# Side steps behind TensorE's last queued block, spaced by products; two norms' roots moved to VectorE

## The chip, the cores and the metric

The kernel runs on one core of a Trainium2 chip. The metric is the device time of one execution in microseconds (us), taken as the median of several runs. Engines: PE is TensorE (PEld its weight loads), DVE is VectorE, ACT is ScalarE, POOL is GpSimd, SP is SyncE, whose queue issues nearly all DMAs here. L96 means line 96 of the kernel before.

## The reference, cut to what matters

One decoder layer on 512 prompt tokens and 8 x 8 sample tokens (576 columns in all), float32. A normalised input `h` is projected by `w_in` (1024 x 6656) and feeds three branches, which sigmoid gates merge:

```
u = ca * sigmoid(cb);  c = causal_dwconv31(u);  c = silu(layernorm(c));  p_conv = c @ w_conv_out
q,k,v,f -> HGRN2, 4 heads of 128x128 state;  o = rmsnorm(o) * silu(hgate);  p_hg = o @ w_hg_out
s = qm @ mem_k^T / sqrt(128);  om = softmax(s) @ mem_v;  p_mem = om @ w_mem_out
out = (g0*p_conv + g1*p_hg + g2*p_mem) @ w_out        (then RMSNorms and a dense SwiGLU FFN)
```

The sample tokens attend to 8 caches of 256 keys and values per head, which are loaded from HBM.

## The kernel before, in words

Every large product is made of three passes over pairs of rounded high and low parts (`mm3`, L94 to L97), so that PE is the busiest engine. Until about 545 us the kernel works through a list of **tasks** (L1068 to L1097). Most tasks are one **block**: 16 calls of `mm3` (8 rows of weights for each of two groups of 256 and 320 tokens), whose two results lie in two of the four PSUM buffers with the tag `mm` and are then read by ACT or DVE. A `p_conv` or `p_mem` task is 8 calls. The order of tasks that matters here: four convolution inputs, keys and values, four queries (`q_task`), eight `gate_conv`, `hgate(0)`, `hq(0)`, `hf(0)`, `hgate(1..3)`, eight `p_conv`, then the gates and outputs of the memory branch with heads 1 and 2 between them, then `gate_hg` with head 3, then `p_hg`.

Beside the blocks run **side steps**, written as generators: the convolution's taps and its layer norm (`conv_taps`, `conv_tail`, in the queue `convq`), attention of the prompt and the heads (`attn_prompt`, `hg_decay`, `hg_main`, in `side`) and the sample tokens' attention (`attn_sample`, in `sampq`). After each task `pump(conv, ns)` takes `conv` steps from `convq` and `ns` from the two others. This sets the order in which instructions are written down; a planner with costs of its own then orders each engine's queue, taking what it holds to be ready, earlier lines first.

What is named below:

- `conv_tail` (L435): sums over channels (L454 to L456 on DVE, L461 on PE), centring (L465), squares (L468, L471, L472), the variance of each token by ten one-column products (L477, PSUM buffer `ps`), copies (L480, L481), a root `rsqrt` (L133) on POOL, five diagonal tiles on DVE (L487), five products that spread the root over all partitions (L489, PSUM buffers `pr`), and per channel group the scaling (L494, L495), sigmoid (L498), L499, L500 and the split into high and low parts, the first write of which is ACT L102 into a fresh big buffer `hl` (L491).
- `attn_sample` (L628): eight units of key transposes (L643), copies (L644) and scores (L649); the softmax (L597 to L603); transposes of the probabilities (L658, a PSUM buffer `ps`) and their copy (L660); products with the cached values (L671, PSUM buffer `ops`, once per group of four sequences); a copy `oo` (L676), transposes (L679) and splits. The values are loaded by SP (L632), two in advance.
- `hq(0)` takes a big buffer for head 0 (`hg_alloc`, L750); its two results are read by ACT L770 and DVE L771, the latter writing into that big buffer. `hf(0)` writes there as well (ACT L764, L765).
- `hg_main` (L835): head norm with squares (L903), sums (L904), a root on POOL, L909, transposes (L915) and the gated output (L922).
- Pools: `S` (8 big buffers), `x` (5), `tb` (3), and in PSUM `mm` (4) and `sd` (4, for all side products). A tile takes a buffer of its tag's ring at its first write.

Of the kernel before, what the change touches and what calls it, by code (L numbers as in the profile page):

```python
# [42 lines left out]
def tile_decoder_layer(  # L43
# [14 lines left out]
    pps = ctx.enter_context(tc.tile_pool(name="pps", bufs=4, space=PSUM))  # L58
    pd = ctx.enter_context(tc.tile_pool(name="pd", bufs=5, space=bass.MemoryType.DRAM))

    seq, last = [0], {}

    def nm(s):
        seq[0] += 1
# [26 lines left out]
    def f32(ap):  # L91
        return ap.bitcast(F32)

    def mm3(out, whi, wlo, xhi, xlo, start, stop, more=False):  # L94
        T.matmul(out, lhsT=whi, rhs=xhi, start=start, stop=False, skip_group_check=more)  # L95
        T.matmul(out, lhsT=whi, rhs=xlo, start=False, stop=False, skip_group_check=more)  # L96
        last["mm"] = T.matmul(out, lhsT=wlo, rhs=xhi, start=False, stop=stop, skip_group_check=more)  # L97

    def split(hi, lo, src, scale=None, eng=None):

        if scale is None:
            A.activation(hi, src, AF.Copy)  # L102
            (eng or V).tensor_tensor(lo, src, f32(hi), op=ALU.subtract)  # L103
        else:
            ins = A.activation(hi, src, AF.Identity, scale=scale)  # L105
            ins2 = V.scalar_tensor_tensor(out=lo, in0=src, scalar=scale, in1=f32(hi), op0=ALU.mult,  # L106
                                          op1=ALU.subtract)
            return ins, ins2
# [201 lines left out]
    h = (hhi, hlo)  # L310
    convq, side, sampq = deque(), deque(), deque()

    def step(q):
        while q:
            try:
                next(q[0])
                return
            except StopIteration:
                q.popleft()

    def pump(nc_=1, ns=1):
# [12 lines left out]
    g0, g1 = GRP
    junk = big()
# [99 lines left out]
    def conv_tail():  # L435
        last = tmp(512)
        for j in range(4):
            A.activation(last[:, P * j:P * j + 30], uext[:, j, 512:542], AF.Copy)
            A.activation(last[:, P * j + 32:P * j + 96].rearrange("p (b t) -> p b t", b=NB),
                         usamp(j)[:, :, 30:38], AF.Copy)  # L440
        ps, psb = sdb(), sdb()
        for j in range(4):
            T.transpose(ps[:30, P * j:P * j + P], last[:, P * j:P * j + 30], ident)
            T.transpose(psb[:64, P * j:P * j + P], last[:, P * j + 32:P * j + 96], ident)
        l2, l3 = tmp(512), tmp(512)
        A.activation(l2[:30, :], ps[:30, :], AF.Copy)
# [12 lines left out]
        for g in range(2):  # L459
            t0, n = GRP[g]  # L460
            T.matmul(pm[g][:, :n], lhsT=ones, rhs=s[:, t0:t0 + n], start=True, stop=True)  # L461
        for j in range(4):
            for g in range(2):
                t0, n = GRP[g]
                V.tensor_tensor(ca[:, j, t0:t0 + n], ca[:, j, t0:t0 + n], pm[g][:, :n], op=ALU.subtract)  # L465
            if j == 0:
                s = tmp()
                A.activation(s, ca[:, j], AF.Square)  # L468
            else:
                sq = tmp()  # L470
                A.activation(sq, ca[:, j], AF.Square)  # L471
                V.tensor_tensor(s, s, sq, op=ALU.add)  # L472
            yield
        ps = sdb()
        for t in range(5):
            m = P if t < 4 else 64
            T.matmul(ps[:m, 2 * t:2 * t + 1], lhsT=s[:, P * t:P * t + m], rhs=ones[:, 0:1], start=True, stop=True)  # L477
        vs = tiny()
        V.memset(vs, 1.0)
        V.tensor_copy(vs[:, 0:4], ps[:, 0:8].rearrange("p (a b) -> p a b", b=2)[:, :, 0])  # L480
        V.tensor_copy(vs[:64, 4:5], ps[:64, 8:9])  # L481
        r = rsqrt(vs[:, 0:5], 5, 1.0)
        pr = [sdb(), sdb()]
        for t in range(5):
            m = P if t < 4 else 64
            dg = tmp(P)
            V.tensor_scalar(dg[:m, :m], ident[:m, :m], r[:m, t:t + 1], 512.0, op0=ALU.mult, op1=ALU.mult)  # L487
            o = pr[0][:, P * t:P * t + P] if t < 4 else pr[1][:, :64]
            T.matmul(o, lhsT=ones[:m, :], rhs=dg[:m, :m], start=True, stop=True)  # L489
        yield  # L490
        hl = big(FR).rearrange("p (s j t) -> p s j t", s=2, j=4)  # L491
        hi, lo = hl[:, 0], hl[:, 1]
        for j in range(4):
            V.tensor_tensor(ca[:, j, :512], ca[:, j, :512], pr[0], op=ALU.mult)  # L494
            V.tensor_tensor(ca[:, j, 512:], ca[:, j, 512:], pr[1][:, :64], op=ALU.mult)  # L495
            g, b = cT[:, j, 32:33], cT[:, j, 33:34]
            sg = tmp()
            A.activation(sg, ca[:, j], AF.Sigmoid, scale=g, bias=b)  # L498
            V.tensor_scalar(ca[:, j], ca[:, j], g, b, op0=ALU.mult, op1=ALU.add)  # L499
            V.tensor_tensor(ca[:, j], ca[:, j], sg, op=ALU.mult)  # L500
            split(hi[:, j], lo[:, j], ca[:, j])
            yield
        chl.append((hi, lo))
# [124 lines left out]
    def attn_sample():  # L628
# [29 lines left out]
                T.transpose(ps[:, 256 * g + P * mh:256 * g + P * mh + P], pr[:, g, P * mh:P * mh + P], ident)  # L658
        pT = xtile()[:, :512]
        A.activation(pT, ps, AF.Copy)  # L660
        yield
        for g in range(2):
            ops = sdb()
            for j in range(4):
                vj, u = vcs.popleft(), 4 * g + j + 2
                if u < 8:
                    vcs.append(load(cache_mem_v, *units[u]))
                for mh in range(2):
                    for b in range(4):
                        c = 256 * g + P * mh + 32 * b  # L670
                        T.matmul(ops[32 * b:32 * b + 32, P * j:P * j + P], lhsT=pT[:, c:c + 32],  # L671
                                 rhs=vj[:, 2 * b + mh, :], start=mh == 0, stop=mh == 1)
                if j % 2:
                    yield
            oo = tmp(512)
            A.activation(oo, ops, AF.Copy)  # L676
            ps = sdb()
            for j in range(4):
                T.transpose(ps[:, P * j:P * j + P], oo[:, P * j:P * j + P], ident)  # L679
            c0 = SEQ + 32 * g  # L680
            for j in range(4):
                src = ps[:, P * j:P * j + P].rearrange("p (b i t) -> p b i t", b=4, i=4)[:, :, j, :]
                hi, lo = (mem["om"][:, s, j, c0:c0 + 32].rearrange("p (b t) -> p b t", b=4) for s in range(2))
                split(hi, lo, src)
            yield
# [87 lines left out]
    def hg_decay(j):  # L773
# [56 lines left out]
        A.activation(d["kEs"][64:, :], ps[64:, :P], AF.Copy)  # L830
        d["scaled"] = scaled
        G.memset(d["sc"], 0.0)
        yield

    def hg_main(j):  # L835
        d = hg[j]
# [11 lines left out]
        for t in range(4):  # L848
# [3 lines left out]
            else:  # L852
# [11 lines left out]
        vm = tmp(512)  # L864
        V.tensor_tensor(vm[64:].rearrange("p (b v) -> p b v", b=4), vs.unsqueeze(1).to_broadcast([64, 4, P]),
                        m4[64:].unsqueeze(2).to_broadcast([64, 4, P]), op=ALU.mult)
        yield
        ps = sdb()
        for t in range(4):
            c = P * t  # L870
# [33 lines left out]
        V.reduce_sum(ss[:, 0:4], sq.rearrange("p (t v) -> p t v", t=4), axis=AX.X)  # L904
        sq = tmp(P)
        A.activation(sq[:64, :], obs[:64, :P], AF.Square, accum_out=ss[:64, 4:5])
        r = rsqrt(ss[:, 0:5], 5, 1.0 / P)
        on = d["on"]
        V.tensor_tensor(on[:, :512].rearrange("p (t v) -> p t v", t=4), ob.rearrange("p (t v) -> p t v", t=4),  # L909
                        r[:, 0:4].unsqueeze(2).to_broadcast([P, 4, P]), op=ALU.mult)  # L910
        V.tensor_scalar(d["ons"][:64, :], obs[:64, :P], r[:64, 4:5], None, op0=ALU.mult)
        yield
        pT, pTs = sdb(), sdb()
        for t in range(4):
            T.transpose(pT[:, P * t:P * t + P], on[:, P * t:P * t + P], ident)  # L915
# [2 lines left out]
        if j == 0:  # L918
# [3 lines left out]
        V.scalar_tensor_tensor(out=og[:, :512], in0=pT, scalar=g, in1=gt[:, :512], op0=ALU.mult, op1=ALU.mult)  # L922
        V.scalar_tensor_tensor(out=og[:, 512:], in0=pTs[:, :64], scalar=g, in1=gt[:, 512:], op0=ALU.mult,
                               op1=ALU.mult)
        split(hg["og"][:, 0, j], hg["og"][:, 1, j], og)
        yield

        Ds = PP[:, 512:576].rearrange("p (b t) -> p b t", b=NB)[:, :, 7]
# [17 lines left out]
    def win(c):  # L946
        return wcols(w_in, c, P)
# [111 lines left out]
        return norm_group(xtb, 0, hhi, hlo, *g1, junk=junk[:, D:2 * D], eng=A, fills=8)  # L1059

    def hgate(j):
        add(hg_task(j), win(C_HG + P * j), ns=4)

    def hf(j):
        add(hq_task(j), win(C_HQ + P * j), ns=4)
        add(hf_task(j), win(C_HF + P * j), ns=4)

    for j in range(4):  # L1068
        add(conv_task(j), win(C_CB + P * j), win(C_CA + P * j), conv=1)
# [9 lines left out]
    for j in range(1, 4):  # L1079
        hgate(j)  # L1080
    for n in range(8):
        add(p_conv(n), *([wcols(w_conv_out, P * n, 256)] if n % 2 == 0 else []), conv=2, ns=3)
    for n in range(0, 8, 2):
        add(gate_mem(n), win(C_GL + 2 * D + P * n), ns=4)
        add(gate_mem(n + 1), win(C_GL + 2 * D + P * n + P), ns=4)
        add(p_mem(n), wcols(w_mem_out, P * n, 256), ns=3)
        add(p_mem(n + 1), ns=3)
# [467 lines left out]
```

## Time and profile before

| | us |
|---|---|
| median of 3 runs (1004.88 to 1005.20) | 1005.19 |
| the profiled execution | 1005.55 |
| its span from first to last instruction | 1003.8 |
| PE busy in it | 986.9 |
| DVE, ACT, POOL busy | 693.3, 433.5, 33.5 |

The profiled execution is 1.75 us longer than its span. A timeline row gives start, length, engine, line, operation, tiles, shapes, the number of merged instructions, and in brackets how long the engine stood idle before it and what ended that. Since matmuls overlap, a busy PE can still be slower than PE at its peak.

### The profile page before, as it was taken

To read this page: it belongs to the slowest core of one execution; us is meant where nothing else is said; L and a number is where in the kernel's file an instruction comes from. 1 tells how busy PE (TensorE), PEld (TensorE's weight loads), DVE (VectorE), ACT (ScalarE), POOL (GpSimd) and SP (SyncE) were. 2 spreads that over 40 slices of the span, in tenths; PEclk is the share of its full clock that TensorE was granted. 3 is DMA by queue.
4 is the path that set the end of the run, shared out by engine and by line. 5 is a ranking of instruction groups with operands and counts; after the bars stand their busy time and mean duration, and the time that the engine had idled before them with its cause. 6 is when DMAs were issued, how large, how long until landed. Compare 5 with 4: busy or idle time off the path is not lost.

```text
span 1003.8 us, 16880 instructions
## 1 busy us (share of the span) xinstructions
PE 986.9 (98%) x6915; PEld 924.0 (92%) x6915; DVE 693.3 (69%) x1235; ACT 433.5 (43%) x766; POOL 33.5 (3%) x127
## 2 busy tenths in 40 slices
PE   8999999999899999999999999999999999999997
PEld 7997899889699999999999779999999999999995
DVE  6689997485875365566548788878777876813715
ACT  6544346574621232223234466344444544614612
POOL 1120000000101001001000000000000000000000
PEclk9999999999999999999999999999999999999999
DMA  8415421543743222222323615023232333321302
GB/s 244 140 64 194 121 80 47 148 132 107 207 134 95 84 85 75 76 87 65 95 77 134 181 64 178 1 85 114 77 104 85 96 115 137 139 81 54 128 20 95
DMA packets 125931, 106.55 MB, mean 106 GB/s; under 512 B 3208, under 2 KB 110244, under 8 KB 125846
## 3 DMA queue, kind: packets, MB, share of 16 engines
q1 hardware_dynamic: 125854, 105.48, 33.9%
q8 instruction: 54, 0.88, 0.4%
q14 instruction: 23, 0.19, 0.1%
HBM read 97.15 MB, written 8.68 MB: 105 GB/s over the span
## 4 chain that ended last, share of the span: by engine, by line
PE 82%; DVE 7%; DMA 5%; ACT 2%; issue 2%; POOL 1%; SPq 0%; DVEq 0%; ACTq 0%
PE mm L96 18%; PE mm L95 18%; PE mm L97 18%; PE sd L96 3%; PE sd L95 3%; PE sd L97 3%; PE sd L1465 2%; PE sd L1466 2%; PE sd L1467 2%; DVE wl L103 1%; DMA x<-in_cache_mem_v_dram 1%; DMA wr<-in_w_ffn_gate_dram 1%; DVE S L428 1%; DMA wr<-in_w_out_dram 1%; DVE S L106 1%
## 5 line engine op out<-in xcount | busy, mean ns | idle before, releaser
L96 PE MATMUL mm<-S,wh 128*128 128x320 f32 (+1 forms) x1216 | 363.3, 299 | 0.3 <-DVE S L106 0.3
L95 PE MATMUL mm<-S,wh 128*128 128x320 f32 (+1 forms) x1216 | 361.5, 299 | 1.5 <-ACT S L105 1.0
L97 PE MATMUL mm<-S,wl 128*128 128x320 f32 (+1 forms) x1216 | 362.4, 299 | 0.0
L95 PEld LDWEIGHTS mm<-S,wh 128*128 128x128 f32 x1216 | 227.9, 188 | 6.5 <-issue 2.6
L97 PEld LDWEIGHTS mm<-S,wl 128*128 128x128 f32 x1216 | 228.3, 188 | 3.9 <-issue 3.5
L96 PEld LDWEIGHTS mm<-S,wh 128*128 128x128 f32 x1216 | 228.6, 188 | 3.6 <-issue 1.5
L103 DVE TENSOR_TENSOR wl<-wr,wh 128x1024 fp32r<-128x1024 f32 x98 | 119.6, 1221 | 127.9 <-ACT wh L102 127.5
L102 ACT ACTIVATE wh<-wr 128x1024 fp32r<-128x1024 f32 x98 | 103.6, 1059 | 224.9 <-PE mm L96 174.1
L428 DVE SCALAR_TENSOR_TENSOR S<-S,cT,S 128x512 f32<-128x512 f32 x120 | 89.9, 749 | 2.5
L96 PE MATMUL mm<-S,wq 128*128 128x288 f32 x216 | 63.7, 295 | 0.0
L97 PE MATMUL mm<-S,wq 128*128 128x288 f32 x216 | 63.7, 295 | 0.0
L96 PE MATMUL sd<-S,wq 128*128 128x288 f32 x216 | 63.6, 295 | 0.0
L95 PE MATMUL sd<-S,wq 128*128 128x288 f32 x216 | 63.6, 294 | 0.0
L95 PE MATMUL mm<-S,wq 128*128 128x288 f32 x216 | 63.6, 294 | 0.0
L97 PE MATMUL sd<-S,wq 128*128 128x288 f32 x216 | 63.1, 294 | 0.0
L102 ACT ACTIVATE wq<-ws 128x1024 fp32r<-128x1024 f32 x36 | 37.9, 1056 | 37.8 <-PE mm L96 35.2
L103 DVE TENSOR_TENSOR wq<-ws,wq 128x1024 fp32r<-128x1024 f32 x36 | 43.7, 1217 | 3.0 <-ACT wq L102 3.0
L103 DVE TENSOR_TENSOR S<-S,S 128x1152 fp32r<-128x1152 f32 (+3 forms) x46 | 44.1, 986 | 1.8 <-ACT S L102 1.7
L102 ACT ACTIVATE S<-S 128x1152 fp32r<-128x1152 f32 (+3 forms) x46 | 38.1, 864 | 6.9 <-DVE S L521 4.9
L97 PEld LDWEIGHTS mm<-S,wq 128*128 128x128 f32 x216 | 40.6, 188 | 0.0
L96 PEld LDWEIGHTS sd<-S,wq 128*128 128x128 f32 x216 | 40.5, 188 | 0.0
L95 PEld LDWEIGHTS sd<-S,wq 128*128 128x128 f32 x216 | 40.5, 188 | 0.0
(371 smaller groups left out, 1689.5 us busy)
## 6 DMA issues: line engine op xcount, KB each, us to landing
wr<-in_w_in_dram SPq DMA_DIRECT2D x52, 512.0 KB
wr<-in_w_ffn_down_dram SPq DMA_DIRECT2D x22, 512.0 KB
S<-in_w_ffn_gate_dram SPq DMA_DIRECT2D x9, 1024.0 KB
S<-in_w_ffn_up_dram SPq DMA_DIRECT2D x9, 1024.0 KB
x<-in_x_prompt_dram SPq DMA_DIRECT2D x8, 512.0 KB
wr<-in_w_mem_kv_dram SPq DMA_DIRECT2D x8, 512.0 KB
x<-in_cache_mem_k_dram SPq DMA_DIRECT2D x8, 512.0 KB
x<-in_cache_mem_v_dram SPq DMA_DIRECT2D x8, 512.0 KB
```

The lines of the kernel that those rows point to most:

```text
L95: T.matmul(out, lhsT=whi, rhs=xhi, start=start, stop=False, skip_group_check=more)
L96: T.matmul(out, lhsT=whi, rhs=xlo, start=False, stop=False, skip_group_check=more)
L97: last["mm"] = T.matmul(out, lhsT=wlo, rhs=xhi, start=False, stop=stop, skip_group_check=more)
L102: A.activation(hi, src, AF.Copy)
L103: (eng or V).tensor_tensor(lo, src, f32(hi), op=ALU.subtract)
L106: ins2 = V.scalar_tensor_tensor(out=lo, in0=src, scalar=scale, in1=f32(hi), op0=ALU.mult, op1=ALU.subtract)
L428: queue(V.scalar_tensor_tensor(out=dp, in0=src, scalar=w, in1=dp, op0=ALU.mult, op1=ALU.add))
L1465: T.matmul(pa[ti], lhsT=ah, rhs=w[0][:, kk, :], start=f == 0, stop=False)
L1466: T.matmul(pa[ti], lhsT=al, rhs=w[0][:, kk, :], start=False, stop=False)
L1467: T.matmul(pa[ti], lhsT=ah, rhs=w[1][:, kk, :], start=False, stop=f == NF - 1)
```

## The change

`step` keeps for each queue a count from which its next step may be written: a step yields a number, and the queue's next step is held until that many more calls of `mm3` have been written (`drain` ignores it). `pump` writes its steps inside `tc.issue_after` of the last product written, so their PE instructions are queued behind that product and no earlier. Numbers are given behind the squares, the diagonal tiles, the probabilities' transposes, each second value product, the copy `oo`, the heads' transposes, queries and norm. The spreading of the convolution's root becomes one product of 512 columns and one of 64, from one diagonal tile. Two roots, `conv_tail`'s and `hg_main`'s, go from POOL to DVE. `hgate`, `hq` and `hf` pump up to three and six steps (`conv=3, ns=6`); `p_conv`, `gate_mem`, `p_mem` and `gate_hg` get `ns=6`.

```diff
     def mm3(...):
...
+        last["n"] += 1
...
-    def step(q):
+    def step(q, force=False):
         while q:
+            if not force and last["n"] < due.get(id(q), 0):
+                return
             try:
-                next(q[0])
+                due[id(q)] = last["n"] + (next(q[0]) or 0)
                 return
...
     def pump(nc_=1, ns=1):
-        for _ in range(nc_):
-            step(convq)
-        for i in range(ns):
-            if sampq and i >= 2:
+        with tc.issue_after(last["mm"].ins):
+            for _ in range(nc_):
+                step(convq)
+            for _ in range(ns - 2 if sampq and ns > 2 else ns):
+                step(side)
+            for _ in range(2 if ns > 2 else 0):
                 step(sampq)
-            else:
-                step(side)
@@ conv_tail @@
-            yield
+            yield 8 if j == 3 else 0
         ps = sdb()
...
-        r = rsqrt(vs[:, 0:5], 5, 1.0)
-        pr = [sdb(), sdb()]
+        r = rsqrt(vs[:, 0:5], 5, 1.0, eng=V)
+        dg = tmp()
         for t in range(5):
             m = P if t < 4 else 64
-            dg = tmp(P)
-            V.tensor_scalar(dg[:m, :m], ident[:m, :m], r[:m, t:t + 1], 512.0, op0=ALU.mult, op1=ALU.mult)
-            o = pr[0][:, P * t:P * t + P] if t < 4 else pr[1][:, :64]
-            T.matmul(o, lhsT=ones[:m, :], rhs=dg[:m, :m], start=True, stop=True)
+            V.tensor_scalar(dg[:m, P * t:P * t + m], ident[:m, :m], r[:m, t:t + 1], 512.0, op0=ALU.mult, op1=ALU.mult)
+        yield 8
+        pr = [sdb(), sdb()]
+        T.matmul(pr[0], lhsT=ones, rhs=dg[:, :512], start=True, stop=True)
+        T.matmul(pr[1][:, :64], lhsT=ones[:64, :], rhs=dg[:64, 512:], start=True, stop=True)
         yield
@@ attn_sample @@
         A.activation(pT, ps, AF.Copy)
-        yield
+        yield 8
...
-                if j % 2:
-                    yield
+                yield 8 * (j % 2)
             oo = tmp(512)
             A.activation(oo, ops, AF.Copy)
+            yield 8
@@ hg_decay: the last yield; hg_main: the second @@
-        yield
+        yield 8
@@ hg_main, norm @@
-        r = rsqrt(ss[:, 0:5], 5, 1.0 / P)
+        r = rsqrt(ss[:, 0:5], 5, 1.0 / P, eng=V)
...
-        yield
+        yield 16
...
-        add(hg_task(j), win(C_HG + P * j), ns=4)
+        add(hg_task(j), win(C_HG + P * j), conv=3, ns=6)
```

## Rows read from the trace of the kernel before

**Rows 1.** The page: its first part, and of its fourth the chain's shares by engine.
```profile
PE 986.9 (98%) x6915; PEld 924.0 (92%) x6915; DVE 693.3 (69%) x1235; ACT 433.5 (43%) x766; POOL 33.5 (3%) x127
...
PE 82%; DVE 7%; DMA 5%; ACT 2%; issue 2%; POOL 1%; SPq 0%; DVEq 0%; ACTq 0%
```

**Rows 2.** PE's waits between 30 and 560 us: who waited for whom, us in total, times, longest.
```profile
PE sd L671 <- DMA x<-in_cache_mem_v_dram: 1.5, 2, 1.0
PE sd L489 <- DVE tb L487: 1.2, 1, 1.2
PE sd L671 <- ACT x L660: 0.7, 1, 0.7
PE mm L95 <- DVE S L771: 0.5, 1, 0.5
```

**Rows 3.** Busy time by stretch: stretch and its length, then PE, PEld, DVE, ACT, POOL busy (instructions), granted clock, DMA share, GB/s.
```profile
254.00:264.00 10.00, 7.22 (x88) 5.46 (x87) 7.47 (x21) 8.90 (x15) 0.42 (x1) 0.83 0.55 166
264.00:276.00 12.00, 10.86 (x130) 10.12 (x131) 11.97 (x23) 7.02 (x17) 0.58 (x1) 1.00 0.97 248
276.00:545.00 269.00, 269.00 (x2069) 258.00 (x2068) 161.49 (x314) 76.05 (x136) 16.71 (x64) 1.00 0.30 91
...
258.00:260.00 2.00, 1.21 (x14) 0.63 (x16) 2.00 (x3) 1.45 (x4) 0.00 (x0) 0.88 0.02 4
260.00:263.00 3.00, 2.55 (x48) 1.95 (x40) 2.96 (x9) 2.99 (x4) 0.00 (x0) 0.51 0.86 261
```

**Rows 4.** Timeline of PE, 234 to 276 us: the side products, and the first product of the block that follows.
```profile
234.43 1.13 PE L461 MATMUL sd<-tb,ones 128*128 128x256 f32 x4
...
235.40 0.60 PE L619 MATMUL sd<-ident,x 128*128 128x128 f32 x4
...
239.19 1.88 PE L624 MATMUL sd<-x,S 128*128 128x512 f32 x4
...
247.71 1.03 PE L643 MATMUL sd<-ident,x 128*128 128x128 f32 x8
...
248.58 1.16 PE L477 MATMUL sd<-ones,tb 128*128 128x1 f32 x10
...
255.28 0.83 PE L489 MATMUL sd<-tb,ones 128*128 128x128 f32 x6
257.28 0.85 PE L489 MATMUL sd<-tb,ones 128*128 128x128 f32 x4 [1.17 <-DVE tb L487]
258.24 0.83 PE L658 MATMUL sd<-ident,x 128*128 128x128 f32 x4
259.76 2.79 PE L671 MATMUL sd<-x,x 128*32 128x128 f32 x48 [0.69 <-ACT x L660]
...
264.17 0.39 PE L95 MATMUL mm<-S,wh 128*128 128x256 f32 x1 [0.47 <-DVE S L771]
...
273.11 0.65 PE L671 MATMUL sd<-x,x 128*32 128x128 f32 x16 [0.98 <-DMA x<-in_cache_mem_v_dram]
```

**Rows 5.** Timeline of ACT: the sigmoid of `hq(0)`'s second result, a split of weights and the softmax's last step, the first write into `hl`, the first write of `hf(0)`'s.
```profile
245.04 0.43 ACT L770 ACTIVATE mt<-mm 128x320 f32<-128x320 f32 x1
...
256.73 1.05 ACT L102 ACTIVATE wh<-wr 128x1024 fp32r<-128x1024 f32 x1
257.68 0.90 ACT L603 ACTIVATE x<-x,tn 128x256 f32<-128x256 f32 x2
...
263.32 0.68 ACT L102 ACTIVATE S<-S 128x576 fp32r<-128x576 f32 x1
...
264.68 0.36 ACT L764 ACTIVATE S<-mm 128x256 f32<-128x256 f32 x1
```

**Rows 6.** Timeline of DVE: the first copy of the variance, the first two diagonal tiles, the first three scalings, and the reading of `hq(0)`'s first result.
```profile
249.77 0.16 DVE L480 COPY tn<-sd 128x4 f32<-128x4 f32 x1 [3.37 <-PE sd L477]
...
254.05 0.57 DVE L487 TENSOR_SCALAR tb<-ident,tn 128x128 f32<-128x128 f32 x2
...
258.96 1.88 DVE L494 TENSOR_TENSOR S<-S,sd 128x512 f32<-128x512 f32 x3
...
263.70 0.41 DVE L771 TENSOR_TENSOR S<-mm,mt 128x256 f32<-128x256 f32 x1
```

**Rows 7.** Timeline of POOL: the first and the last of the 14 instructions of the convolution's root, and the one behind it.
```profile
250.09 0.20 POOL L144 TENSOR_SCALAR tn<-tn 128x5 f32<-128x5 f32 x1 [192.49 <-DVE tn L481]
...
253.71 0.20 POOL L153 TENSOR_TENSOR tn<-tn,tn 128x5 f32<-128x5 f32 x1
253.85 0.58 POOL L782 MEMSET S<- 128x576 f32 x1
```

**Rows 8.** Timeline of DVE at the kernel's end: the first and the last of the four instructions of one round of the same root there, on three columns.
```profile
987.84 0.16 DVE L150 TENSOR_TENSOR tn<-tn 128x3 f32<-128x3 f32 x1
...
988.44 0.16 DVE L153 TENSOR_TENSOR tn<-tn,tn 128x3 f32<-128x3 f32 x1
```

**Rows 9.** Timelines: of SP, the issue of the eighth unit's keys and of four value loads; of PE, the first scores of the prompt's attention; of ACT, the reading of the first query block's second result.
```profile
236.38 0.45 SPq L632 DMA_DIRECT2D x<-in_cache_mem_k_dram  x1
...
260.90 5.37 SPq L632 DMA_DIRECT2D x<-in_cache_mem_v_dram  x4
...
129.72 1.03 PE L611 MATMUL sd<-S 128*128 128x256 f32 x4
...
130.74 0.37 ACT L589 ACTIVATE S<-mm 128x256 f32<-128x256 f32 x1
```

More of the change, by code (lines that the diff above doesn't have):

```diff
@@ L59, in tile_decoder_layer @@
     pd = ctx.enter_context(tc.tile_pool(name="pd", bufs=5, space=bass.MemoryType.DRAM))
-    seq, last = [0], {}
+    seq, last = [0], {"n": 0}
     def nm(s):
@@ L97, in mm3 @@
         last["mm"] = T.matmul(out, lhsT=wlo, rhs=xhi, start=False, stop=stop, skip_group_check=more)
+        last["n"] += 1
     def split(hi, lo, src, scale=None, eng=None):
         if scale is None:
-            A.activation(hi, src, AF.Copy)
-            (eng or V).tensor_tensor(lo, src, f32(hi), op=ALU.subtract)
+            ins = A.activation(hi, src, AF.Copy)
+            return ins, (eng or V).tensor_tensor(lo, src, f32(hi), op=ALU.subtract)
         else:
@@ L311, in tile_decoder_layer @@
     convq, side, sampq = deque(), deque(), deque()
-    def step(q):
+    due = {}
+    def step(q, force=False):
         while q:
+            if not force and last["n"] < due.get(id(q), 0):
+                return
             try:
-                next(q[0])
+                due[id(q)] = last["n"] + (next(q[0]) or 0)
                 return
@@ L321, in pump @@
     def pump(nc_=1, ns=1):
-        for _ in range(nc_):
-            step(convq)
-        for i in range(ns):
-            if sampq and i >= 2:
+        with tc.issue_after(last["mm"].ins):
[4 more added lines that the diff above has]
+            for _ in range(2 if ns > 2 else 0):
                 step(sampq)
-            else:
-                step(side)
     def drain(q):
         while q:
-            step(q)
+            step(q, True)
     g0, g1 = GRP
@@ L866, in hg_main @@
                         m4[64:].unsqueeze(2).to_broadcast([64, 4, P]), op=ALU.mult)
-        yield
+        yield 8
         ps = sdb()
@@ L911, in hg_main @@
         V.tensor_scalar(d["ons"][:64, :], obs[:64, :P], r[:64, 4:5], None, op0=ALU.mult)
-        yield
+        yield 16
         pT, pTs = sdb(), sdb()
@@ L924, in hg_main @@
                                op1=ALU.mult)
-        split(hg["og"][:, 0, j], hg["og"][:, 1, j], og)
+        last["head"] = split(hg["og"][:, 0, j], hg["og"][:, 1, j], og)
         yield
@@ L1061, in hgate @@
     def hgate(j):
-        add(hg_task(j), win(C_HG + P * j), ns=4)
+        add(hg_task(j), win(C_HG + P * j), conv=3, ns=6)
     def hf(j):
-        add(hq_task(j), win(C_HQ + P * j), ns=4)
-        add(hf_task(j), win(C_HF + P * j), ns=4)
+        add(hq_task(j), win(C_HQ + P * j), conv=3, ns=6)
+        add(hf_task(j), win(C_HF + P * j), conv=3, ns=6)
     for j in range(4):
@@ L1081, in tile_decoder_layer @@
     for n in range(8):
-        add(p_conv(n), *([wcols(w_conv_out, P * n, 256)] if n % 2 == 0 else []), conv=2, ns=3)
+        add(p_conv(n), *([wcols(w_conv_out, P * n, 256)] if n % 2 == 0 else []), conv=2, ns=6)
     for n in range(0, 8, 2):
[L1084 to L1087, printed above, removed]
+        add(gate_mem(n), win(C_GL + 2 * D + P * n), ns=6)
+        add(gate_mem(n + 1), win(C_GL + 2 * D + P * n + P), ns=6)
+        add(p_mem(n), wcols(w_mem_out, P * n, 256), ns=6)
+        add(p_mem(n + 1), ns=6)
         if n == 0:
@@ L1092, in tile_decoder_layer @@
     for n in range(8):
-        add(gate_hg(n), win(C_GL + D + P * n), ns=3)
+        add(gate_hg(n), win(C_GL + D + P * n), ns=6)
         if n == 0:
```

## The prediction

> **What bounds the kernel now.** I read the page first: PE is busy 98% of the span and holds 82% of the chain that ended last [rows 1], so only what moves PE's stream moves the time. Then PE's waits between 30 and 560 us: the side steps' share is four waits, 3.9 us in all, all near one place [rows 2]. The busy time by stretch says where: 10.00 - 7.22 and 12.00 - 10.86, so 3.9 us idle between 254 and 276 us, and none at all in the 269 us that follow, through all four heads [rows 3]. In the same place the granted clock falls: 0.88 over 2 us and 0.51 over 3 us are 0.5 + 2.9 = 3.4 us at the lower of its two levels (1.2 against 2.4 GHz), after PE had stood idle [rows 3]. So whatever the change does for PE, it does in this stretch; at best it wins about 4 us and a little of the clock's loss, 0.5%.
>
> The timelines show why PE stands there. No block's product runs until L95 at 264.17, and that one waited for DVE L771 [rows 4]: of the four `mm` buffers two hold the results of `hq(0)`, two those of `hf(0)`. L771 had its sigmoids by 245.5 (245.04 + 0.43) and DVE was not full [rows 3], yet it came at 263.70, and L764 of `hf(0)` at 264.68: both just behind ACT's first write into `hl` at 263.32 [rows 5, 6]. All three write fresh `S` buffers, and `hl` stands first in the program. The `sd` buffers behave alike: L619 of the fourth prompt head follows L461 directly (235.40 after 234.43), and the variance L477, whose squares were long done, follows the last key transposes L643 directly (248.58 after 247.71) [rows 4]. I read from this: **a tag's buffers are given out in the program's order of first writes, and a tile that isn't ready holds back those behind it.** So PE's stall ends when the convolution's tail writes `hl`: a chain from L477 at 248.58 to L95 at 264.17.
>
> **The change, part by part.** *Holding back to the last queued product.* L477 is written behind `gate_conv(3)` but runs after the last product of `hq(0)`, six blocks on (its result is read at 245.04) [rows 4, 5]: an edge to a product that PE passed long ago moves nothing. The one place I find where a side product ran ahead of its block is the first query: L611 at 129.72, the block's second result read at 130.74 [rows 9]. It moves by some 1 us beside full PE work: 0, at most 1.0 if the whole chain shifts with it.
>
> *The order of the steps.* Following the queues by hand, the old order after `gate_conv(3)` is: centring, **variance, root, spreading**, softmax, **probabilities' transposes**. The new 8 behind the squares holds the variance until `gate_conv(4)`, while softmax and transposes stay with `gate_conv(3)`. So in the `sd` ring L658 now stands ahead of L477, and the first L671 ahead of the spreading. By the rule above L477 can't start before L658, which waits for the softmax: 258.24, the second pair behind the second L603 (257.68 + 0.90 = 258.58) [rows 4, 5]. I take 258.6 between the pairs; 257.2 if the weights' split (1.05, 256.73) lets L603 by, 259.1 behind all four [rows 4, 5]. What is queued behind it: on DVE the copies, root and scalings, then L771; on PE nothing else is free, as every block waits for an `mm` buffer.
>
> *The chain from L477 to L95, new.* L477 itself 1.16 (2.3 at the lower clock) [rows 4]. From its end (249.74) to the root's first step (250.09) 0.35 [rows 4, 7]. The root: 14 steps. On POOL they took 3.9 (250.09 to 253.91 and the hand-over), 0.28 apart [rows 7]; on DVE dependent steps of three columns start 0.20 apart ((988.44 - 987.84)/3) [rows 8], so 2.8. Bounds: 2.2, if each took only its own 0.16 [rows 8], and 3.9 as on POOL. The diagonal tiles 5 x 0.285 = 1.4, as the first two [rows 6]. Spreading by one 512-column product: L624 has two such in 1.88, so 0.94 (1.9 at the lower clock) [rows 4]; the old ten instructions with their wait took 255.28 to 258.13, 2.9, but PE has nothing else to do then, so only this chain counts. Scaling to the first write of `hl`: 263.32 - 258.96 = 4.36, of which two of three L494 (1.25) needn't stand ahead [rows 5, 6]; I take 3.7 between 3.1 and 4.36. From `hl` to L95: 264.17 - 263.32 = 0.85 [rows 4, 5]. Sum: 1.16 + 0.35 + 2.8 + 1.4 + 0.94 + 3.7 + 0.85 = 11.2, so L95 starts at 258.6 + 11.2 = 269.8 in place of 264.17: **+5.6**.
>
> DVE and POOL read SBUF through one port that they share, so work moved from one to the other may win nothing, says the Trainium skill (Perfetto Trace Analysis, Optimizing Scalar/DVE Operations). The rows differ: 0.20 a step against 0.28 [rows 7, 8]. By the skill the root would stay at 3.9 and the sum be 1.1 higher.
>
> *Clock.* Before, the lower level fell in while PE waited anyway. Now PE stands nearly idle for some 4 us just before the blocks resume; if they start at the lower level for as long as before, 3.4 us, half of that is lost: between 0 and 1.7, I take 0.9 [rows 3].
>
> *The sample values.* Their steps go from two values to one; eight loads are still issued by SP two in advance, the four of the second half from 260.90 on [rows 9]. Their order against the weights stays. L671 waited 0.98 for one at 273.11 [rows 4]; 5 us later it would be there: -1.0 (0 at least). Head 0's state load and store move by a block or two behind them; `x` buffers come in the same order.
>
> *Heads.* Roots of 14 steps on DVE, 70 with the convolution's, 14 us at 0.20; DVE is busy 161 of 269 us there and PE never waits [rows 3, 8]: 0. If DVE filled up, L771 and its like would hold `mm` buffers. POOL's memset L782 no longer stands behind a root (253.85 after 253.71) [rows 7], but nothing waits for it. That some head steps are written a block later: 0 for the same reason.
>
> *Fewer, larger side runs, more steps per pump:* 0, since the planner still places them when ready.
>
> **Sum:** 5.6 + 0.9 - 1.0 + 0 = +5.5. The profiled execution took 1005.55, 0.36 over the median; so 1011.0 there and 1010.7 as a median. With all low bounds: 5.6 - 1.4 - 0.6 - 0.6 - 1.0 = +2.0; with all high ones 5.6 + 0.5 + 1.1 + 1.1 + 1.0 + 0.7 + 1.7 + 1.0 = +12.7.
>
> **Rivals.** *Faster: the variance keeps its place.* If the `sd` ring doesn't hold L477 behind L658, it starts at 248.58 as now, and the shorter chain (11.2 for 15.6) lets L95 start at 259.8, 4.4 us earlier: 1000.8. For it: the waits that go (L487's 1.2 [rows 2]) lie in the chain. Against: the three pairs of rows above, which agree. It is decided at L477: 264.17 - 11.2 = 253.0 is the start at which nothing is won or lost; I have it at 258.6.
>
> *Same: the chain turns round but starts early.* The last keys were issued at 236.38 [rows 9] and the softmax's chain hangs on them. If the new order of queues brings keys, scores and softmax some 5 us forward, L658 and L477 come near 253 and the time stays at 1005.2. For it: SP and the rings are full of such shifts. Against: up to `gate_conv(3)` the order of steps is the old one, so nothing I see brings the keys forward.
>
> **How the numbers follow.** A difference below 0.2% (2 us) can't be told from none by a measurement of this kernel. Forecast (L477 behind L658): 0.62, 1010.7, its own range 1007.2 (all low) to 1015. Faster rival: 0.23, around 1000.8, or up to 1003 where part of it is eaten. Same: 0.15. The range of 8 in 10 reaches from 1001.0, into the faster case, to 1013.5; about 0.1 lies on either side.
>
> **What would show it.** Right: PE's side products in the order L643, L658, L477, and L477 after 257; L477 to L95 in some 11 us; PE idle between 254 and 270 near 9 us instead of 2.8 in 254 to 264; the lower clock at the blocks' restart; L771 still just behind the first write of `hl`; no wait in the heads. Wrong: L477 ahead of L658, or L771 free of `hl`; then the rule of the rings is not what held PE, and the faster rival takes over. A root step far from 0.20 on DVE, or a PE wait behind 276 us, would make single terms wrong.

## The result and the profile after

| us | before | after |
|---|---|---|
| median (4 runs each) | 1005.04 (1004.41 to 1005.20) | 1013.61 (1012.89 to 1015.49) |
| ratio, 95% interval | | 1.0089 [1.0072, 1.0107] |
| profiled execution, its span | 1005.55, 1003.8 | 1015.49, 1013.8 |
| PE busy, PE idle (span less busy) | 986.9, 16.9 | 989.8, 24.0 |

The kernel became 8.6 us slower. Of the runs further down, one execution of e5 (4847 us) and one of e9 (3397 us) were slow ones and are left out of their medians. Lines of the kernel after lie up to 7 below those of before: L477 became L483, L489 L495 and L496, L494 L501, L658 L665, L671 L678, L764 L771, L771 L778; L95 stayed.

The page, the parts that answer to [rows 1]:
```profile
PE 989.8 (98%) x6909; PEld 926.6 (91%) x6909; DVE 705.6 (70%) x1305; ACT 434.0 (43%) x766; POOL 17.8 (2%) x57
...
PE 83%; DVE 7%; DMA 4%; ACT 2%; issue 2%; POOL 1%; SPq 1%; DVEq 0%; ACTq 0%
```
Of the 10.0 us between the two spans, 7.1 are idle time of PE and 2.9 are busy time: the same products took longer. PE's waits between 30 and 560 us, for [rows 2]:
```profile
PE mm L95 <- DVE S L778: 4.9, 1, 4.9
PE sd L665 <- ACT x L610: 4.1, 1, 4.1
PE sd L678 <- ACT x L667: 0.7, 1, 0.7
```
Two long waits are new: one for the softmax ahead of its transposes, one for the query gate ahead of the next block. L671's wait for a sample value is gone. Busy time by stretch, columns as in [rows 3]:
```profile
254.00:264.00 10.00, 5.24 (x51) 4.42 (x53) 4.35 (x21) 6.14 (x10) 0.00 (x0) 0.70 0.42 130
264.00:276.00 12.00, 6.86 (x61) 5.46 (x54) 10.23 (x28) 6.68 (x12) 0.00 (x0) 0.78 0.75 201
276.00:545.00 269.00, 268.57 (x2109) 257.54 (x2108) 169.91 (x360) 73.01 (x132) 4.36 (x9) 1.00 0.30 92
266.00:272.00 6.00, 1.35 (x19) 0.67 (x18) 4.97 (x12) 2.91 (x5) 0.00 (x0) 0.96 1.14 301
272.00:278.00 6.00, 5.76 (x26) 5.76 (x27) 6.00 (x13) 4.01 (x10) 0.00 (x0) 0.50 0.10 24
```
Between 254 and 276 PE is idle 4.76 + 5.14 = 9.9 us, against 3.9 before; from 276 to 545 it lost 0.4. The last line shows the restarted blocks at a granted clock of 0.50, the lower of the two levels. PE's timeline there, for [rows 4]:
```profile
248.06 1.03 PE L650 MATMUL sd<-ident,x 128*128 128x128 f32 x8
...
258.68 0.69 PE L665 MATMUL sd<-ident,x 128*128 128x128 f32 x2 [4.07 <-ACT x L610]
259.16 2.01 PE L483 MATMUL sd<-ones,tb 128*128 128x1 f32 x10
261.10 0.69 PE L665 MATMUL sd<-ident,x 128*128 128x128 f32 x2
262.47 2.60 PE L678 MATMUL sd<-x,x 128*32 128x128 f32 x48 [0.69 <-ACT x L667]
265.31 1.10 PE L495 MATMUL sd<-tb,ones 128*128 128x512 f32 x2 [0.24 <-DVE tb L492]
...
272.24 0.58 PE L95 MATMUL mm<-S,wh 128*128 128x256 f32 x1 [4.90 <-DVE S L778]
...
279.49 1.74 PE L678 MATMUL sd<-x,x 128*32 128x128 f32 x56
```
The variance L483 no longer follows the key transposes L650; it stands between the two pairs of the probabilities' transposes, 10.6 us later than in [rows 4]. The first block restarts at 272.24, not 264.17. DVE and then ACT in the chain between, for [rows 5, 6]:
```profile
261.21 0.16 DVE L486 COPY tn<-sd 128x4 f32<-128x4 f32 x1 [3.12 <-PE sd L483]
...
261.46 0.17 DVE L145 TENSOR_SCALAR tn<-tn 128x5 f32<-128x5 f32 x1
...
264.29 1.03 DVE L492 TENSOR_SCALAR tb<-ident,tn 128x128 f32<-128x128 f32 x5
266.45 2.48 DVE L501 TENSOR_TENSOR S<-S,sd 128x512 f32<-128x512 f32 x4 [1.12 <-PE sd L495]
268.85 0.60 DVE L502 TENSOR_TENSOR S<-S,sd 128x64 f32<-128x64 f32 x4
...
271.77 0.42 DVE L778 TENSOR_TENSOR S<-mm,mt 128x256 f32<-128x256 f32 x1
```
```profile
258.12 0.91 ACT L610 ACTIVATE x<-x,tn 128x256 f32<-128x256 f32 x2 [0.23 <-DVE tn L608]
...
269.09 2.38 ACT L505 ACTIVATE tb<-S,cT 128x576 f32<-128x576 f32 x3 [5.37 <-DVE S L502]
271.40 0.68 ACT L103 ACTIVATE S<-S 128x576 fp32r<-128x576 f32 x1
...
272.75 0.36 ACT L771 ACTIVATE S<-mm 128x256 f32<-128x256 f32 x1
```
Again the query gate's reading (L778, 271.77) and `hf(0)` (L771, 272.75) come just behind the first write of `hl` (L103, 271.40).

### The profile page after: what moved, and what is told of

The parts are those of the page before. It is cut to its first block, busy times and chain, and to the rows that moved or that the text cites. A ratio compares the mean times of both kernels' runs of the same rounds, so it can differ in the third digit from the quotient of the medians.

```text
span 1013.8 us, 16861 instructions
## 1 busy us (share of the span) xinstructions
PE 989.8 (98%) x6909; PEld 926.6 (91%) x6909; DVE 705.6 (70%) x1305; ACT 434.0 (43%) x766; POOL 17.8 (2%) x57
## 4 chain that ended last, share of the span: by engine, by line
PE 83%; DVE 7%; DMA 4%; ACT 2%; issue 2%; POOL 1%; SPq 1%; DVEq 0%; ACTq 0%
PE mm L96 19%; PE mm L95 19%; PE mm L97 18%; PE sd L96 3%; PE sd L95 3%; PE sd L97 3%; PE sd L1472 2%; PE sd L1473 2%; PE sd L1474 2%; DVE wl L104 1%; DMA wr<-in_w_ffn_gate_dram 1%; DVE S L434 1%; DMA wr<-in_w_in_dram 1%; DMA wr<-in_w_out_dram 1%; DVE S L104 1%
## 5 line engine op out<-in xcount | busy, mean ns | idle before, releaser
L95 PE MATMUL mm<-S,wh 128*128 128x320 f32 (+1 forms) x1216 | 363.0, 301 | 6.4 <-DVE S L778 4.9
L95 PEld LDWEIGHTS mm<-S,wh 128*128 128x128 f32 x1216 | 229.3, 189 | 11.4 <-DVE S L778 5.0
L103 ACT ACTIVATE wh<-wr 128x1024 fp32r<-128x1024 f32 x98 | 103.6, 1059 | 219.0 <-PE mm L96 172.4
L95 PE MATMUL sd<-S,wq 128*128 128x288 f32 x216 | 63.6, 294 | 0.0
L95 PE MATMUL mm<-S,wq 128*128 128x288 f32 x216 | 63.6, 294 | 0.0
L103 ACT ACTIVATE wq<-ws 128x1024 fp32r<-128x1024 f32 x36 | 37.9, 1056 | 39.1 <-PE mm L96 34.2
L103 ACT ACTIVATE S<-S 128x1152 fp32r<-128x1152 f32 (+3 forms) x46 | 38.1, 864 | 6.0 <-DVE S L528 5.4
L95 PEld LDWEIGHTS sd<-S,wq 128*128 128x128 f32 x216 | 40.5, 188 | 0.0
```

The costliest lines, as they stand in the source:

```text
L103: ins = A.activation(hi, src, AF.Copy)
```

## The experiments

Theory: the variance's place in the `sd` ring makes the chain late, and PE feels it because `hl` stands ahead of head 0's buffer in the `S` ring. Rivals: other parts of the change, the clock, DVE.

| run | median us | ratio to before [95%] | variance | L95 restarts |
|---|---|---|---|---|
| after | 1013.61 | 1.0089 [1.0072, 1.0107] | 259.16 | 272.24 |
| e1 | 1005.82 | 1.0009 [0.9999, 1.0018] | 248.78 | 264.14 |
| e2 | 1009.08 | 1.0041 [1.0027, 1.0056] | 248.52 | 267.48 |
| e3 | 1014.82 | 1.0095 [1.0078, 1.0112] | 258.13 | 273.04 |
| e4 | 1000.59 | 0.9957 [0.9942, 0.9972] | 248.46 | no stall |
| e5 | 1009.43 | 1.0050 [1.0034, 1.0066] | 260.64 | stall at 278.7 to 285.83 |
| e6 | 1015.50 | 1.0110 [1.0094, 1.0125] | 257.90 | 273.69 |
| e7 | 1012.48 | 1.0075 [1.0060, 1.0090] | 258.69 | 271.78 |
| e8 | 1002.09 | 0.9968 [0.9955, 0.9981] | as e4 | no stall |
| e9 | 1014.99 | 1.0098 [1.0082, 1.0115] | 258.72 | 273.62 |
| e10 | 1013.74 | 1.0084 [1.0069, 1.0099] | 258.08 | 272.75 |
| e11 | 999.43 | 0.9943 [0.9926, 0.9959] | 248.18 | no stall |
| e12 | 1005.80 | 1.0009 [1.0000, 1.0018] | 248.33 | 263.93 |
| e13 | 1012.53 | 1.0076 [1.0061, 1.0091] | 258.23 | 270.35 |
| e14 | 1008.70 | 1.0037 [1.0024, 1.0050] | 248.01 | 262.24 |

**e1, both steps kept early** (the changed kernel):
```diff
-            yield 8 if j == 3 else 0
+            yield
...
-        yield 8
         pr = [sdb(), sdb()]
```


> The changed kernel with two of its new step borders taken out: a plain yield behind the squares, and none between the diagonal tiles and the spreading. Theory (place in the sd ring): variance near 248.6 us and spreading both ahead of the softmax's transposes; root on DVE 2.8, so the spreading by 254.5 to 255.5, L95 restarts at 260 to 262 instead of 272.24; PE idle in 254 to 264 under 2 us; no long lower clock behind it; 1001 to 1003 us. Rival (the loss comes from the other parts: holding back to the last product, larger side runs, sample steps): still 1010 or more.

Without these two borders 7.7 of the 8.6 us are gone, and the rest can't be told from the kernel before. But the forecast of 1001 to 1003 missed; the variance ran at 248.78 and the blocks still restarted at 264.14. DVE shows why:
```profile
252.06 0.17 DVE L154 TENSOR_TENSOR tn<-tn,tn 128x5 f32<-128x5 f32 x1
253.44 0.69 DVE L603 TENSOR_REDUCE tn<-sd 128x2 f32<-128x512 f32 x1 [1.21 <-PE sd L655]
254.05 0.15 DVE L151 TENSOR_TENSOR tn<-tn 128x5 f32<-128x5 f32 x1
...
257.70 1.23 DVE L104 TENSOR_TENSOR wl<-wr,wh 128x1024 fp32r<-128x1024 f32 x1 [0.78 <-ACT wh L103]
258.85 1.88 DVE L500 TENSOR_TENSOR S<-S,sd 128x512 f32<-128x512 f32 x3
```
In the middle of the root DVE waits for the softmax's scores (L603), since its queue runs in order; the root takes 250.23 to 254.82, 4.6 us, longer than the 3.9 on POOL. Then the scaling L500 stands behind a weights' split, which waits for ACT.

**e2, only the spreading late** (the changed kernel):
```diff
-            yield 8 if j == 3 else 0
+            yield
```


> The changed kernel with the 8 behind the squares alone taken out; the border ahead of the spreading stays. Theory: variance near 248.6, but the spreading's two buffers stand behind the transposes' one, so it starts only at some 258.7 to 259.5; then 0.94 to 1.1 for it, 3.7 to 4.95 to the first write of hl, 0.85 to L95: 264.2 to 266.4, nothing to 2 us behind the kernel before; with the clock 1005 to 1008 us. If only the variance's place counted: 1001 to 1003. If neither border counts: 1010 or more.

The spreading fell between the two pairs of transposes, as forecast, at 258.13, and `hl` was first written at 264.14. The time is 1 us over the forecast, as PE's next side products then waited for a sample value:
```profile
264.66 1.08 PE L678 MATMUL sd<-x,x 128*32 128x128 f32 x16 [3.01 <-DMA x<-in_cache_mem_v_dram]
266.47 1.08 PE L678 MATMUL sd<-x,x 128*32 128x128 f32 x16 [0.73 <-DMA x<-in_cache_mem_v_dram]
```

**e3, one border added to the kernel before:**
```diff
                 V.tensor_tensor(s, s, sq, op=ALU.add)
             yield
+        yield
         ps = sdb()
```


> The kernel before with one empty yield behind the squares, so that the variance's step is taken one call later, behind the softmax; the root stays on POOL, the spreading stays ten instructions. Theory: the variance falls behind the first transposes as in the changed kernel, 258.6 to 259.2, and the old chain of 15.6 us follows: L95 at 273.5 to 275, 9 to 11 us later than in the kernel before; less 1.0 for the sample values and up to 3 for the clock: 1012 to 1018 us. Rival (the edit alone is harmless): 1004 to 1006.

One empty border costs 9.9 us by the medians of its own runs (1014.82 against 1004.96): the whole loss, without any other part of the change.
```profile
258.13 2.01 PE L478 MATMUL sd<-ones,tb 128*128 128x1 f32 x10
...
273.04 0.58 PE L95 MATMUL mm<-S,wh 128*128 128x256 f32 x1 [2.81 <-DVE S L772]
```

**e4, `hl` taken early in the kernel before:**
```diff
+        hl = big(FR).rearrange("p (s j t) -> p s j t", s=2, j=4)
+        V.memset(f32(hl[:, 0, 0, 0:1]), 0.0)
         s = tmp()
         V.tensor_tensor(s, ca[:, 0], ca[:, 1], op=ALU.add)
...
-        hl = big(FR).rearrange("p (s j t) -> p s j t", s=2, j=4)
```


> The kernel before with hl taken, and one column of it set to 0 by DVE, at the tail's sums, long before the variance; nothing else changes. Theory (what PE waits for is hl's place ahead of the head's buffer): the first product of the query gate L771 follows its sigmoids near 246 to 250, the blocks run on through 254 to 264, PE idle there under 0.5 us instead of 2.8, no lower clock there; 1000 to 1002 us, though variance and spreading come no earlier. Rival (the blocks wait for the chain itself, or for DVE): L771 still near 263, 1005.

The memory and the chain are the same; only the place of `hl`'s first write differs. DVE reads the two results of `hq(0)` at once, where [rows 6] has the first at 263.70, and PE is full:
```profile
240.99 0.42 DVE L772 TENSOR_TENSOR S<-mm,mt 128x256 f32<-128x256 f32 x1
...
246.20 0.48 DVE L772 TENSOR_TENSOR S<-mm,mt 128x320 f32<-128x320 f32 x1
```
```profile
254.00:264.00 10.00, 10.00 (x77) 9.81 (x77) 6.91 (x18) 7.56 (x14) 0.58 (x1) 1.00 0.37 110
```
So the rule of the rings holds for `S`: PE waited for an order of buffers, not for room or for the convolution. The Trainium skill (Perfetto Trace Analysis, Identifying Performance Opportunities) says that consistent bubbles, the same gap repeating, can mean that SBUF or PSUM has no room for the next tile. The gap here is a single one; it too hangs on a tile's buffer, and it goes without a byte more.

**e5, `hl` taken early in the changed kernel:**
```diff
+        hl = big(FR).rearrange("p (s j t) -> p s j t", s=2, j=4)
+        V.memset(f32(hl[:, 0, 0, 0:1]), 0.0)
         s = tmp()
...
-        hl = big(FR).rearrange("p (s j t) -> p s j t", s=2, j=4)
```


> The changed kernel with hl taken, and one column of it set to 0 by DVE, at the tail's sums; all its new borders stay. Theory: the late variance costs only through hl's place. It still stands behind the first transposes (257 or later), but the query gate's L778 follows its sigmoids near 246 to 250, the blocks run through 254 to 272, PE idle there under 1 us, no lower clock; 1000 to 1002 us. Rival (the late variance itself or the other parts of the change cost the time): 1008 or more.

Half a miss. The stall in 254 to 264 went (PE 10.00 of 10.00), but a second came:
```profile
285.83 1.33 PE L95 MATMUL mm<-S,wh 128*128 128x256 f32 x4 [7.12 <-ACT S L103]
```
That is the first `p_conv`, which needs `hl`'s contents. With the blocks running, head 0's steps got ahead of the variance's copies on DVE (L488 at 269.38), and the scaling began at 278.38. The late variance has two prices; `hl`'s place was only the earlier.

**e6, roots back on POOL** (the changed kernel):
```diff
-        r = rsqrt(vs[:, 0:5], 5, 1.0, eng=V)
+        r = rsqrt(vs[:, 0:5], 5, 1.0)
...
-        r = rsqrt(ss[:, 0:5], 5, 1.0 / P, eng=V)
+        r = rsqrt(ss[:, 0:5], 5, 1.0 / P)
```


> The changed kernel with the convolution's and the heads' roots back on POOL. Theory (each step its own time): root 3.9 for 2.8, so L95 at 273.2 to 273.6 instead of 272.24 and 1014.0 to 1015.5 us; no wait in the heads. Rival (the two engines share a port, nothing won by DVE): L95 at 272.2, 1013.6. Other rival (the DVE roots cost the heads time): below 1013.

The root took 259.98 to 263.74, 3.8, against 2.83 (261.46 to 264.29), and the restart came 1.45 later, though softmax and variance came 1.3 earlier. Time and restart lie at the upper end of the theory's, but the lower clock, now from 258.3 to 278.8 without a break, is in the difference too: the two spreading products took 2.8 in place of 1.5. The part of the root can't be told apart by the time.

**e7, the second hole filled** (the changed kernel):
```diff
+        fill = sdb()
+        for _ in range(4):
+            T.matmul(fill, lhsT=ones, rhs=dg[:, :512], start=True, stop=True)
```


> The changed kernel with four more 512-column products into a spare sd buffer behind the spreading, which nothing reads: some 3.8 us of PE work in the 4.9 us in which PE stands idle ahead of L95. Theory (the lower granted clock at the restart follows that idling): L95 still near 272.2 to 272.6, but the blocks behind it at the upper level, so up to 3 us less: 1010.5 to 1012.5. Rival (the level has another reason): the stretch of lower clock stays, 1013.6 or a little more.

```profile
266.81 3.70 PE L499 MATMUL sd<-tb,ones 128*128 128x512 f32 x8
271.78 0.39 PE L95 MATMUL mm<-S,wh 128*128 128x256 f32 x1 [1.27 <-DVE S L781]
```
In this execution the clock stayed at its upper level after the restart (L95's first product 0.39, not 0.58), and its span is 4.2 us shorter than the changed kernel's profiled one. The medians differ by 1.1 only, and their intervals overlap. The changed kernel's profiled run had a mean granted clock of 0.991, its other three 0.993 to 0.994, and all four runs of this one 0.993 to 0.994 too. So the time lies in the theory's range, but that the filling took the lower level away is not shown.

**e8, e4 with a border behind `oo`:**
```diff
             A.activation(oo, ops, AF.Copy)
+            yield
```


> The kernel before with hl taken early as in the run above, and a border between the copy of the sample values' sums and their transposes. Theory: L680's wait of 1.3 us behind 276 goes, the rest stays: 999 to 1000 us against 1000.6. Rival (the border moves the wait to another side step): 1000.6.

The wait of 1.3 us stayed: the planner put the transposes in the same place. Nothing won; the median lies 1.5 us above e4's, with overlapping intervals.

**e9, spreading products swapped** (the changed kernel):
```diff
+        T.matmul(pr[1][:, :64], lhsT=ones[:64, :], rhs=dg[:64, 512:], start=True, stop=True)
         T.matmul(pr[0], lhsT=ones, rhs=dg[:, :512], start=True, stop=True)
-        T.matmul(pr[1][:, :64], lhsT=ones[:64, :], rhs=dg[:64, 512:], start=True, stop=True)
```


> The changed kernel with its two spreading products in the other order, the 64-column one first. Theory (the scaling took 4.95 us to the first write of hl, for 3.7 predicted, because DVE's scalings of the last 64 columns, L502, waited for the second product behind 16 others): the scalings alternate, hl's first write comes 1 to 1.6 us earlier, L95 at 270.6 to 271.3; 1012 to 1012.7 us. Rival (the sigmoids or the table load set it): 272.2 and 1013.6.

A miss. DVE now ran all four 64-column scalings first and then all four of 512, and both products moved behind all 64 value products; `hl` was first written at 272.11. Swapping the producers did not make the scalings alternate. Nor had L502 waited for its product in the changed kernel, as the theory said: DVE had no idle time between L501 and L502.

**e10, both holes filled** (e7, and in `attn_sample` behind the softmax; `mx` are its maxima):
```diff
+        fill = sdb()
+        for _ in range(4):
+            T.matmul(fill[:2, :], lhsT=mx[:, 0:2], rhs=ca[:, 0, 0:512], start=True, stop=True)
```


> The changed kernel with both idle stretches of PE filled by products into spare sd buffers that nothing reads: four of 512 columns behind the softmax's maxima (two rows each, some 3.8 us), four behind the spreading. Theory (the lower clock follows the idling, and it costs the variance 0.85 us and the restart the rest): no lower clock between 250 and 290 at all; variance 1.2 us, L95 at 270.5 to 271.5; 1010.5 to 1012 us. Rival (the clock's share is nothing beyond the second hole): as with one hole filled, 1012.5.

A miss for theory and rival alike. The variance took 1.16, as forecast, but the lower clock came all the same, from 261.55 to 271.79. PE had been busy for 6.53 of the 7.55 us from 254 to 261.55 when the clock fell, and it was busy without a break from 264 on:
```profile
254.00:264.00 10.00, 7.53 (x74) 3.56 (x76) 5.01 (x24) 5.77 (x10) 0.00 (x0) 0.88 0.64 188
264.00:276.00 12.00, 12.00 (x52) 6.70 (x49) 8.00 (x18) 4.29 (x8) 0.00 (x0) 0.68 0.55 151
```
The second fill then took 5.83 in place of 3.70. So "the lower clock follows PE's idling" is too simple. DVE and ACT show something else, about the ring:
```profile
271.79 0.57 DVE L509 TENSOR_SCALAR S<-S,cT 128x576 f32<-128x576 f32 x1
272.28 0.82 DVE L785 TENSOR_TENSOR S<-mm,mt 128x256 f32<-128x256 f32 x2
```
```profile
273.33 0.87 ACT L508 ACTIVATE tb<-S,cT 128x576 f32<-128x576 f32 x1 [2.11 <-PE sd L499]
274.11 0.67 ACT L103 ACTIVATE S<-S 128x576 fp32r<-128x576 f32 x1
```
The third sigmoid waited for the fill, so `hl` was first written at 274.11, and yet the query gate's reading (L785) ran at 272.28 and let PE restart at 272.75. On the chip it did not wait for that write. It stands where the planner put it in DVE's queue, directly behind the tail's second gain (L509), just as L778 follows L506 without idle time in the changed kernel. The rule of the rings acts in the planner's order.

**e11, e1 with `hl` early:**
```diff
+        hl = big(FR).rearrange("p (s j t) -> p s j t", s=2, j=4)
+        V.memset(f32(hl[:, 0, 0, 0:1]), 0.0)
         s = tmp()
...
-        hl = big(FR).rearrange("p (s j t) -> p s j t", s=2, j=4)
```


> All of the change but the two borders around the variance and the spreading, and hl taken at the tail's sums. Theory (without those two borders the change costs nothing, and hl's place was all that held PE): L778 near 246 to 250, no stall in 254 to 276, no lower clock, 999.5 to 1001.5 us, as the kernel before with hl early (1000.59). Rival (the rest of the change costs or wins time by itself): more than 1 us off that.

No stall as before (PE idle 0.5 us between 246 and 290), no lower clock before the kernel's end. The rest of the change costs nothing that could be measured. This is the lowest median of all versions, below both kernels; its interval and e4's overlap.

**e12, e1 with the convolution's root on POOL:**
```diff
-        r = rsqrt(vs[:, 0:5], 5, 1.0, eng=V)
+        r = rsqrt(vs[:, 0:5], 5, 1.0)
```


> The changed kernel with the variance and the spreading kept early as in the first run of this study, and the convolution's root back on POOL, the heads' roots on DVE. There the root on DVE took 250.23 to 254.82, as it stood in line behind the softmax's maxima, which waited for the scores. Theory: on POOL 3.9 again, spreading 0.7 earlier and clear of the weights' split at 257.70, so L95 at 262 to 263.5 instead of 264.14; 1004 to 1005.5 us against 1005.82. Rival (DVE's own steps are what is late): L95 at 264 or later.

A miss. The spreading came 0.84 earlier (255.03 for 255.87) and the restart only 0.2: the scaling waited until 258.71 for the same weights' split, which stands behind the softmax's exponentials on ACT. The root was not what paced this chain.

**e13, the scalings' order set** (the changed kernel; DVE runs blocks 0 and 1, then block 0's gate, then blocks 2 and 3; `one` and `two` are a block's scalings of 512 and 64 columns, `done` the gates):
```diff
+            if j:
+                tc.add_manual_dep(one.ins, two.ins.name, NOSYNC, reason="in pairs")
+            if j > 1:
+                tc.add_manual_dep(one.ins, done[j - 2].ins.name, NOSYNC, reason="behind the pair before")
```


> The changed kernel with the order of the tail's scalings on DVE set: first of block 0 its 512 and its 64 columns, then of block 1, then block 0's gain and gate, and only then the scalings of blocks 2 and 3. Theory (3.7 was predicted and 4.95 measured because all four 512-column scalings, 2.48, stood ahead): first write of hl some 1.2 to 1.7 us earlier, L95 at 270.5 to 271.1 instead of 272.24; 1011.8 to 1012.7 us. Rival (something else paces it): 272 or later, 1013.6.

```profile
265.57 0.69 DVE L502 TENSOR_TENSOR S<-S,sd 128x512 f32<-128x512 f32 x1 [1.18 <-PE sd L495]
```
```profile
266.76 1.63 ACT L510 ACTIVATE tb<-S,cT 128x576 f32<-128x576 f32 x2 [3.97 <-DVE S L507]
269.07 0.68 ACT L103 ACTIVATE S<-S 128x576 fp32r<-128x576 f32 x1 [0.68 <-DVE S L512]
```
From the first scaling to the first write of `hl` 3.50 in place of 4.95: to the first sigmoid 1.19 in place of 2.64, and from there 2.31 in both. L95 at 270.35. Of its 1.9 us, 1.0 is a shorter chain (12.12 from the variance for 13.08; 0.4 was lost again behind `hl`) and 0.9 an earlier softmax. The median is in the theory's range, but its interval overlaps the changed kernel's; the trace shows the gain, the time alone does not.

**e14, the softmax behind the sigmoids** (e12, the softmax two steps later, and its exponentials ordered behind the tail's last sigmoid, `tail_sg`):
```diff
+                tc.add_manual_dep(e.ins, tail_sg[0].ins.name, NOSYNC, reason="behind the sigmoids")
...
+        for _ in range(2):
+            yield
```


> The kernel with variance and spreading early and the convolution's root on POOL (last run of the call before, L95 at 263.93), and the samples' softmax two steps later and its exponentials put behind the tail's four sigmoids on ACT. Theory (there the scaling waited until 258.71 for a weights' split behind the exponentials, and the sigmoids until 260.77 for ACT): the sigmoids start by 258 to 259.5, L95 at 261 to 262.5, PE idle in 254 to 264 about 2 us less; 1002.5 to 1004.3 us. Rival (DVE's scalings themselves need that long): L95 at 263.9, 1005.8.

The restart came at 262.24, as forecast, but the time lies 4.4 us above the forecast's upper end:
```profile
255.65 0.43 PE L495 MATMUL sd<-tb,ones 64*128 64x64 f32 x2
262.24 0.58 PE L95 MATMUL mm<-S,wh 128*128 128x256 f32 x1 [6.15 <-DVE S L781]
```
The softmax's products, which had run in the hole (L664 and L677 of e12, 0.84 + 2.16 between 254 and 264), now ran behind the restart: PE is idle 7.1 of the 44 us from 246 to 290, against 4.5 in e12. The blocks also ran some 5.0 us at the lower level behind the restart, in e12 3.4. So the time of the restart is only a part of the account; what PE does until then, and the clock behind it, are the rest.

Not run: the change without `issue_after`. What it does by itself is not shown, beyond that e11 contains it and shows no cost.

## Why the prediction was right in kind and too small

The mechanism and the sign were right: 1010.7 was predicted and 1013.6 measured, just above the range. Of the 2.9 us between, 0.6 are the later start of the variance, 1.9 the chain behind it, and the rest the clock at the restart. Step by step:

- *The order of the steps.* Right: L650, L665, L483. The variance started at 259.16 for 258.6; e3 shows that this place alone makes the loss, and e4 that PE feels it through `hl`'s place. The prediction's sign of being wrong, "L771 free of `hl`", did come in e10, where the query gate's reading ran 1.8 us ahead of `hl`'s first write: the ring sets the order in DVE's queue, not a wait on the chip. Beyond `hl`'s place the prediction saw nothing; e5 shows a second bound 14 us behind the first restart (285.83 against 272.24).
- *The chain from L477 to L95.* **This is the step that was too small:** 11.2 predicted, 13.08 measured. Variance and its hand-over to the root 2.30 (1.16 + 0.35 predicted; at the lower clock the variance took 2.01); root 2.83 (2.8); diagonal tiles 1.02 (1.4); spreading 1.14 (0.94); from the first scaling to `hl` **4.95** (3.7 taken, 4.36 the upper bound); `hl` to L95 0.84 (0.85). The scaling's term failed where it said that two of the three scalings "needn't stand ahead": DVE's queue held all four of 512 columns ahead of the first of 64 (266.45 to 268.85), and e13 with another order measured 3.50. The second miss in the chain is the lower clock during the variance, 0.8, which stood in the bounds only; the tiles, 0.4 shorter than taken, hid a part of both. So L95 came 8.1 us later, not 5.6.
- *Clock.* 0.9 taken, 1.7 the bound. In the profiled execution the blocks ran from 272.24 to some 278.4 at the lower level, at half their rate: 3.1 us. By it the terms give 8.1 + 3.1 - 1.0 = 10.2, against 10.0 between the spans. Against the median's 8.6, the same sum leaves 1.5 for the clock; the other three runs had a mean granted clock of 0.993 to 0.994, the profiled one 0.991. The bound was wrong because it took the length of one such stretch before, 3.4, for the longest; here two of 6.8 came.
- *The sample values.* Right: no wait at 279.49, -1.0. e2 shows the other side: with the products earlier the same loads cost 3.7.
- *The root on DVE.* 0.20 a step, as taken from [rows 8]. The Trainium skill (Perfetto Trace Analysis, Optimizing Scalar/DVE Operations) says that moving work between DVE and POOL might not help, as they share a port. Here it did help: 2.83 on DVE, 3.8 on POOL in e6. What the prediction left out is that DVE's queue is in order: in e1 the root stood 1.8 us behind the softmax's maxima and its wait, and POOL was quicker there (e12, 0.84).
- *Holding back to the last queued product; heads; larger side runs.* Right: the first query's scores moved from 129.72 to 130.0, PE lost 0.4 us in 276 to 545, and e11 shows no cost of the rest.
- *The faster rival, 1000.8.* Its mechanism, the variance early, is e1 and e12, and its price was wrong: L95 did not start at 259.8 but at 264.14 and 263.93. In e1 the root took 4.6 for 2.8, and the scaling began 2.98 behind the spreading's start for 0.94 (255.87 to 258.85), as it stood behind the weights' split and ACT's exponentials. Taking the root's part away gained 0.2 (e12), moving the exponentials 1.7 more (e14). The way to 1000 was not a shorter chain but `hl`'s place (e4, e11).

## What to carry to other kernels

Where a planner gives the tiles of one tag their buffers in the program's order, look for the tile that is written late and stands ahead of one that is ready: an early first write of one column was worth 4.4 us here, while a step border put ahead of the late tile cost 9.9. Before moving a small chain to a faster engine, read what stands ahead of it in that engine's queue. And a stall's price is PE's idle time plus what the clock does on the way out, not the shift of the restart alone: work that filled the hole must run somewhere (e14).

## What the runs showed of the hardware

The granted clock was harder to foresee than any queue. The Trainium skill (TensorE: Matmul & The Clock Gate, What's actually happening) says that the level follows how busy PE has been of late. The changed kernel's profiled execution agrees: the level fell near 257.9, after PE had stood idle from 254.6 on, and again near 271.6, after it had stood idle for some 4 us. e10 does not agree with it as read from the busy time: the level fell at 261.55 behind 6.53 busy us of 7.55, and it stayed low to 271.79 with PE busy without a break from 264 on. Why it did so no run here shows. Nor is it shown that filling a hole keeps the level up: e7's profiled execution had no lower level behind the restart, but by their mean granted clocks its runs do not differ from the changed kernel's other three.
